# Selections, small S5 tables, splits on VectorE and a fourth PSUM bank for the a columns of a hybrid S5 and DeltaNet block

## The chip, the cores and the metric

The kernel runs on one core of a Trainium2 chip. The metric is the time on the device of one execution, in microseconds (us); lower is better.

## The reference

One block of a language model on 1024 tokens of width 1024, all in float32: an RMSNorm, one input projection, two branches side by side, an output projection, a gated addition and a last RMSNorm.

```python
a = rms_norm(h, norm_mix_g)
u_s, z_s, q, k, v, z_d, b_raw, a_raw = split(a @ w_in)      # 1024 x 3080
y_s = s5_branch(u_s, ...) * silu(z_s)                       # 32 groups of 16 channels, 64 states
y_d = gated_deltanet_branch(q, k, v, z_d, b_raw, a_raw, ...)  # 4 heads of 128
h = h + concat(y_s, y_d) @ w_out
h = h + sigmoid(h @ w_gate) * rms_norm(p @ w_ple, ple_norm_g)
return rms_norm(h, final_norm_g)
```

The decay of the DeltaNet branch is g = -exp(A_log) * softplus(a_raw + dt_bias), summed along the tokens and then exponentiated. So the four columns a_raw have to come out far more exactly than the rest. S5 is a diagonal state space with complex poles, which needs cosines and sines of multiples of an angle for each state.

## The kernel before

The engines are TensorE (PE in the profile), VectorE (DVE), ScalarE (ACT) and GpSimd (POOL); each works through its own queue in order. SyncE (SP) issues the transfers.

Float32 products are made of three matmuls in the rounded format fp32r: `mm3` multiplies high by high, high by low and low by high parts. `split(hi, lo, raw, e1, e2)` makes the parts: engine e1 copies raw into hi (rounding it), engine e2 subtracts, lo = raw - hi. The input projection goes in 24 weight tiles of 128 output columns (names u, q, k, v, d, z), each loaded by `wtile` into `wr` (one buffer) and split into `wh` and `wl` (two buffers each). The copy is on ACT; the subtraction is on POOL, but for the three tiles in EARLY, where DVE does it. A tile then takes 2 x 8 x 3 matmuls `pj` of 128x512.

The order on PE is written by the kernel itself. A planner keeps a clock of PE cost and a list of chains; each chain yields a number from the table LAT, the time that the other engines are expected to need until its next step, or the name of something that has to be done first. When no chain is due, the planner takes the next piece of filler, in the order of the string FILL: the projection tiles, then g (gram), l (the GLU of S5, matmuls `pg`), o (first half of the output projection, `po`), w, x (second half and the gate). The order on the other engines is made by the framework's scheduler, which lists instructions by a simulated timeline. Once made, all orders are fixed.

The stages, with the times of the profiled execution:

1. 0 to 67 us: the embedding product (`pe`, copied by ACT into e), the squares of x and their sums, `rms` (some fifty tiny DVE operations on the tile rsc), `scale_x` (8 DVE operations), then PE transposes x into `xtp`, and ACT and DVE split that into `ah` and `al`.
2. 67 to 515 us: the a columns (`a_chain`), with projection matmuls as filler and the four batches of S5 in between. The columns are cut into 64 units, 8 in each of 8 blocks b of 128 input channels. `a_prefix(n)`: 3 matmuls of the input by the tile `tg` (a column times a triangle) into a PSUM bank `pT`; ACT adds a large grid constant and writes `tb`, DVE subtracts neighbours back into the bank, ACT writes two more parts into a tile F. `a_sums(n - 2)`: 4 matmuls by `dg` (a column times the identity) onto the same bank, ACT evacuates it into F, four DVE scans (one for each head) add up, and the last sums go to `vst` (even b, an ACT copy) or `se` (odd b, a DVE subtraction). `diag(b)` makes dg and tg by four POOL products per block. The banks `pT` come from the pool MX (3 buffers); the pool MZ (2 buffers) serves S5, the transposes and others.
3. 515 to 660 us: `g_math` (g from the sums, DVE on 32 columns), its transpose `gtp` on PE, prefix sums in rows, `pe5` (PE brings gls and others back into columns, copied by DVE as `cols`), the decay matrices, the substitution that inverts the 32x32 blocks (`subst`, DVE), the doubling to 64 and 128 (`q32`, `d32`, `q64`).
4. 660 to about 780 us: eight chunks of the recurrence (banks `bk`, operands `ktp`, `kdec`, `rr`, `tq`, `v2`), with `pg` and `po` as filler.
5. To 956 us: the rest of `po`, transposes of h, the gate (`pq`), the output.

In an S5 batch (`s5_batch`), POOL builds the table s5tab of 128 cosines and sines for each state by doubling: seven steps of four dependent operations each.

Of the kernel before, what the change touches and what calls it, by code (L numbers as in the profile page):

```python
# [16 lines left out]
P = 128  # L17
# [8 lines left out]
def hymba_block_kernel(ctx: ExitStack, tc: tile.TileContext, A: dict, out: bass.AP, dbg=None):  # L26
# [10 lines left out]
    pm = ctx.enter_context(tc.tile_pool(name="pm", bufs=2, space=PSUM))  # L37
    ps = ctx.enter_context(tc.tile_pool(name="ps", bufs=1, space=PSUM))
    px = ctx.enter_context(tc.tile_pool(name="px", bufs=3, space=PSUM))
    pz = ctx.enter_context(tc.tile_pool(name="pz", bufs=2, space=PSUM))  # L40
    dr = ctx.enter_context(tc.tile_pool(name="dr", bufs=1, space=DRAM))

    def T(name, dt=F32, shape=None):
# [84 lines left out]
    def rsqrt(o, x, e=V):  # L128
        shp = list(x.shape)
        n = "rs" + "x".join(map(str, shp[1:]))  # L130
        hb = dp.tile(shp, I32, tag=n + "h", name="hb")
        t = dp.tile(shp, F32, tag=n + "t", name="rt")
        V.tensor_scalar(out=hb, in0=x.bitcast(I32), scalar1=1, scalar2=None, op0=ALU.logical_shift_right)
        ts(e, o.bitcast(I32), hb, -1.0, MUL, float(0x5F3759DF), ADD)
        for _ in range(3):
            stt(e, t, x, -0.5, o, MUL, MUL)
            tt(e, t, t, o, MUL)
            stt(e, o, t, 1.5, o, ADD, MUL)
# [176 lines left out]
    ud = dr.tile([4, 8, P, P], F32, name="ud")  # L315

    GRID = 24.0
    se = C("se", [P, 4, 8, 4])
    gridc = C("gridc", [P, 2])
    G.memset(gridc[:, 0:1], GRID)  # L320
    G.memset(gridc[:, 1:2], -GRID)
    FT = [fp.tile([P, FW], F32, tag="F", name=f"F{i}") for i in range(4)]
    wah, wal = C("wah", [P, 8, 4], F32R), C("wal", [P, 8, 4])
    V.tensor_copy(out=wah, in_=wba[:, :, 4:8])
    tt(V, wal, wba[:, :, 4:8], wah.bitcast(F32), SUB)

# [23 lines left out]
    rho8 = C("rho8", [P, 16])  # L350

    MAGIC = 12582912.0

    def s5_params():
        bc4 = TV("bc4", F32, [P, 4, 16, 16])
        SP.dma_start(out=bc4, in_=A["bc"])
        Br, Bi, Cr, Ci = (bc4[:, i] for i in range(4))
        pa = T("pa")
        pos = [0]

        def small(w=16):
# [29 lines left out]
        tt(V, k17, k17, k17, MUL)  # L391
        ts(V, pr, k17, -2.0, MUL, 1.0, ADD)
        en = [(small(), small())]
        V.tensor_copy(out=en[0][0], in_=pr[:, :, 8])
        V.tensor_copy(out=en[0][1], in_=pi[:, :, 8])
        tt(V, x17, lrdt.unsqueeze(2).to_broadcast([P, 16, 17]), lvb, MUL)
        act(k17, x17, AF.Exp)
        V.tensor_copy(out=rho8, in_=k17[:, :, 8])
        tt(V, pr, pr, k17, MUL)
        tt(V, pi, pi, k17, MUL)  # L400
        for i in range(1, 7):
            c0, s0 = en[-1]
# [58 lines left out]
    def s5_batch(b):  # L461
# [54 lines left out]
        V.memset(tab[:, 0, :, 0:1], 1.0)  # L516
        V.memset(tab[:, 1, :, 0:1], 0.0)
        for i in range(7):
            n = 1 << i
            cc = en[i][0][:, pp].unsqueeze(1).unsqueeze(3).to_broadcast([P, 2, 4, n])  # L520
            ss = en[i][1][:, pp].unsqueeze(1).unsqueeze(3).to_broadcast([P, 2, 4, n])
            tt(G, tab[:, :, :, n:2 * n], tab[:, :, :, 0:n], cc, MUL)
            tt(G, tb[:, :, :, 0:n], tab[:, :, :, 0:n], ss, MUL)
            tt(G, tab[:, 0, :, n:2 * n], tab[:, 0, :, n:2 * n], tb[:, 1, :, 0:n], SUB)
            tt(G, tab[:, 1, :, n:2 * n], tab[:, 1, :, n:2 * n], tb[:, 0, :, 0:n], ADD)
        yield f"u{b}"
        yield LAT["tab"]
        u = W("u", "p (g c) -> p g c", g=8)
# [59 lines left out]

    def half(w, hf, evac):
# [106 lines left out]
    def a_prefix(n):  # L696
# [20 lines left out]
    def a_sums(n):  # L717
# [7 lines left out]
            d0, d1 = (f[:, 384 * h + x:384 * h + 384:2] for x in range(2))  # L725
            V.tensor_tensor_scan(out=d0, data0=d0, data1=d1, initial=vst[:, i, h:h + 1] if hf else 0.0, op0=ADD, op1=ADD)  # L726
# [444 lines left out]
    def chunk(n):  # L1171
# [161 lines left out]
    def a_chain():  # L1333
        for n in range(66):
# [189 lines left out]
```

## Time and profile before

| | |
|---|---|
| median of 3 runs | 955.9 us (954.72 to 956.91) |
| the profiled execution | 957.75 us, span 956.0 us |
| mean granted clock of TensorE | 0.916 |
| busy: PE, DVE, ACT, POOL | 805.2, 709.2, 489.6, 343.4 us |

The profile gives start and duration of every instruction in one execution, and for an idle stretch of an engine what ended it ("<-"). A row of a group reads: line, engine, operation, written tile <- read tiles, shape, count | busy us, mean ns of one | idle before. A row of a stage gives its window, its length, the busy time of each engine with the number of instructions, the granted clock, and the load of the transfers. A row of the chain of work that ended last, or of the timeline, starts with the start and the duration in us.

### The profile page before, as it was taken

To read this page: it belongs to the slowest core of one execution; us is meant where nothing else is said; L and a number is where in the kernel's file an instruction comes from. 1 tells how busy PE (TensorE), PEld (TensorE's weight loads), DVE (VectorE), ACT (ScalarE), POOL (GpSimd) and SP (SyncE) were. 2 spreads that over 40 slices of the span, in tenths; PEclk is the share of its full clock that TensorE was granted. 3 is DMA by queue.
4 is the path that set the end of the run, shared out by engine and by line. 5 is a ranking of instruction groups with operands and counts; after the bars stand their busy time and mean duration, and the time that the engine had idled before them with its cause. 6 is when DMAs were issued, how large, how long until landed. Compare 5 with 4: busy or idle time off the path is not lost.

```text
span 956.0 us, 12315 instructions
## 1 busy us (share of the span) xinstructions
PE 805.2 (84%) x4338; PEld 649.1 (68%) x4338; DVE 709.2 (74%) x1478; ACT 489.6 (51%) x890; POOL 343.4 (36%) x326
## 2 busy tenths in 40 slices
PE   6479889877798976988998597599579999899996
PEld 3358468756686764876876376488467887778885
DVE  6946968988999878877548859953778754437886
ACT  7457667676696577766555244112355224113332
POOL 0120458676449348522102022101545219502222
PEclk9779989999899898998999798879789999999998
DMA  7430211403122031132102032104445534301211
GB/s 273 154 120 1 88 34 40 110 14 96 37 60 82 34 88 51 23 136 86 66 1 67 22 133 93 40 2 146 108 107 165 194 140 138 129 1 67 88 45 67
DMA packets 67581, 79.93 MB, mean 84 GB/s; under 512 B 23456, under 2 KB 49344, under 8 KB 67520
## 3 DMA queue, kind: packets, MB, share of 16 engines
q1 hardware_dynamic: 67376, 78.89, 25.9%
q8 instruction: 34, 0.56, 0.2%
q14 instruction: 27, 0.22, 0.1%
q10 hardware_dynamic: 144, 0.26, 0.1%
HBM read 57.39 MB, written 21.74 MB: 83 GB/s over the span
## 4 chain that ended last, share of the span: by engine, by line
PE 48%; DVE 27%; ACT 11%; issue 5%; DMA 5%; POOL 4%; SPq 1%; DVEq 0%; ACTq 0%; POOLq 0%
PE pj L111 16%; DVE F L726 9%; PE pq L111 9%; PE pT L111 6%; PE po L111 5%; ACT F L102 5%; DVE s5x L91 3%; PE bk L111 2%; DMA wr<-in_win 2%; DVE cv L99 2%; PE pg L111 2%; DVE pT L91 2%; ACT L102 1%; POOL wgl L91 1%; DVE s5x L554 1%
## 5 line engine op out<-in xcount | busy, mean ns | idle before, releaser
L111 PE MATMUL pj<-ah,wh 128*128 128x512 f32 x384 | 161.8, 421 | 12.3 <-ACT z L102 6.0
L111 PE MATMUL pj<-ah,wl 128*128 128x512 f32 x384 | 156.8, 408 | 0.7 <-POOL wl L91 0.7
L111 PE MATMUL pj<-al,wh 128*128 128x512 f32 x384 | 157.3, 410 | 0.0
L102 ACT ACTIVATE F<-F,gridc 128x512 f32<-128x512 f32 x128 | 115.2, 986 | 0.0
L91 POOL TENSOR_TENSOR wl<-wr,wh 128x1024 fp32r<-128x1024 f32 x21 | 52.2, 2485 | 137.6 <-ACT wh L102 137.6
L111 PEld LDWEIGHTS pj<-ah,wh 128*128 128x128 f32 x384 | 76.7, 200 | 31.9 <-ACT z L102 6.4
L111 PE MATMUL pT<-tg,ah 128*128 128x512 f32 x128 | 58.0, 453 | 47.0 <-ACT F L102 45.6
L726 DVE TENSOR_TENSOR_SCAN F<-F,vst 128x192 f32<-128x192 f32 x128 | 92.9, 784 | 3.2 <-ACT F L102 3.1
L726 DVE TENSOR_TENSOR_SCAN F<-F 128x192 f32<-128x192 f32 x128 | 85.7, 729 | 7.2 <-ACT F L102 7.1
L111 PEld LDWEIGHTS pj<-ah,wl 128*128 128x128 f32 x384 | 75.9, 198 | 19.5 <-POOL wl L91 1.2
L111 PEld LDWEIGHTS pj<-al,wh 128*128 128x128 f32 x384 | 76.4, 199 | 16.4
L91 DVE TENSOR_TENSOR pT<-F 128x512 f32<-128x512 f32 x64 | 51.0, 797 | 47.9 <-ACT F L102 46.4
L111 PEld LDWEIGHTS pT<-tg,ah 128*128 128x128 f32 x128 | 26.3, 205 | 60.7 <-ACT F L102 51.1
L111 PE MATMUL pq<-wgl,hth 128*128 128x512 f32 (+1 forms) x200 | 66.9, 386 | 0.0
L102 ACT ACTIVATE F<-pT 128x512 f32<-128x512 f32 x64 | 55.5, 867 | 2.1 <-PE pT L111 2.1
L99 DVE SCALAR_TENSOR_TENSOR cv<-raw,pk,cv 128x1023 f32<-128x1023 f32 (+2 forms) x36 | 52.9, 1470 | 3.9 <-ACT cv L102 3.8
L91 POOL TENSOR_TENSOR e<-e,pleg 128x1024 f32<-128x1024 f32 x8 | 19.3, 2412 | 97.7 <-ACT jq L102 88.3
L91 DVE TENSOR_TENSOR h<-h,po 128x512 f32<-128x512 f32 x32 | 21.9, 686 | 40.9 <-PE po L111 40.8
L102 ACT ACTIVATE F<-pT,tbl 128x128 f32<-128x128 f32 x128 | 36.5, 372 | 28.4 <-PE pT L111 28.3
L706 POOL COPY F<-tbl 128x4 f32<-128x4 f32 x32 | 16.5, 517 | 84.5 <-DVE pT L91 84.5
L102 ACT ACTIVATE wh<-wr 128x1024 fp32r<-128x1024 f32 x24 | 25.3, 1052 | 37.9 <-DMA wr<-in_win 14.9
L111 PE MATMUL pT<-dg,al 128*128 128x512 f32 x128 | 44.2, 429 | 0.0
(337 smaller groups left out, 2033.5 us busy)
## 6 DMA issues: line engine op xcount, KB each, us to landing
wr<-in_win SPq DMA_DIRECT2D x24, 512.0 KB, 3.7
x<-in_x SPq DMA_DIRECT2D x8, 512.0 KB, 8.1
wr<-in_wout SPq DMA_DIRECT2D x8, 512.0 KB, 4.0
h<-in_x SPq DMA_DIRECT2D x8, 512.0 KB, 4.6
wr<-in_wgate SPq DMA_DIRECT2D x8, 512.0 KB, 3.3
e<-ed SPq DMA_DIRECT2D x8, 512.0 KB, 3.2
out<-h SPq DMA_DIRECT2D x7, 512.0 KB, 2.6
ed<-e SPq DMA_DIRECT2D x6, 512.0 KB, 12.6
```

The lines of the kernel that those rows point to most:

```text
L91: return e.tensor_tensor(out=o, in0=a, in1=b, op=op)
L99: return e.scalar_tensor_tensor(out=o, in0=a, scalar=s, in1=b, op0=op0, op1=op1)
L102: return S.activation(out=o, in_=i, func=f, **k)
L111: return PE.matmul(o, lhsT=l, rhs=r, start=a, stop=z, **k)
L554: V.tensor_tensor_scan(out=flat(w[:, ri]), data0=flat(rh), data1=flat(v[:, ri]), initial=0.0, op0=MUL, op1=ADD)
L706: G.tensor_copy(out=tb[:, :, 0:1], in_=first)
L726: V.tensor_tensor_scan(out=d0, data0=d0, data1=d1, initial=vst[:, i, h:h + 1] if hf else 0.0, op0=ADD, op1=ADD)
```

## The change

Seven edits, in one diff:

1. Banks. The pool MZ becomes two tags, mz0 and mz1, with one buffer each. Units with n % 4 == 3 take mz1 (`own`), and from the first of them until the chain has ended all other users of MZ (S5's) get mz0. So the units rotate over four banks.
2. Selections. dg and tg of a block are made by one POOL `affine_select` each, from wap (high and low part of the columns in one tile), instead of two products each.
3. Tables. Two small tables of 16 and 8 entries for all 16 poles are built once in `s5_params` (28 small POOL operations); a batch makes its 128 entries from them by 8 POOL products and two sums.
4. All 24 subtractions of `wtile` are on DVE (21 were on POOL).
5. The sums of an odd block go to se2 by an ACT copy of the two last columns; one DVE subtraction in `g_math` replaces the 32 small ones.
6. rr, tq and v2 of a chunk lie in the tile of the small tables (rt4), and the scratch of the large `rsqrt` has one buffer.
7. Five numbers of LAT, which move filler on PE.

```diff
-    pz = ctx.enter_context(tc.tile_pool(name="pz", bufs=2, space=PSUM))
+    pz = ctx.enter_context(tc.tile_pool(name="pz", bufs=1, space=PSUM))
...
+    zi = [0, False]
+    def MZ(name, shape=None, own=False):
+        zi[0] = 1 if own else 0 if zi[1] else 1 - zi[0]
+        return pz.tile(shape or [P, 512], F32, tag=f"mz{zi[0]}", name=name)
...
     def diag(b):
-        sh = [P, 4, P]
         res = [T(f"{n}{b}", F32R, [P, 2, 4, P]) for n in ("dg", "tg")]
-        for x, w in enumerate((wah.bitcast(F32), wal)):
-            for o, m in zip(res, (ident, tri)):
-                tt(G, o[:, x], w[:, b, :].unsqueeze(2).to_broadcast(sh), m.unsqueeze(1).to_broadcast(sh), MUL)
+        w = wap[:, b].rearrange("p x h -> p (x h)").unsqueeze(2).to_broadcast([P, 8, P])
+        for o, c in zip(res, (ALU.is_equal, ALU.is_ge)):
+            G.affine_select(out=o.rearrange("p x h c -> p (x h) c"), in_=w, pattern=[[0, 8], [1, P]],
+                            compare_op=c, fill=0.0, base=0, channel_multiplier=-1)
...
+    def rotate(tb, x, i, c, s):
+        n = 1 << i
+        tt(G, tb[:, :, :, n:2 * n], tb[:, :, :, 0:n], c, MUL)
+        tt(G, x[:, :, :, 0:n], tb[:, :, :, 0:n], s, MUL)
+        tt(G, tb[:, 0, :, n:2 * n], tb[:, 0, :, n:2 * n], x[:, 1, :, 0:n], SUB)
+        tt(G, tb[:, 1, :, n:2 * n], tb[:, 1, :, n:2 * n], x[:, 0, :, 0:n], ADD)
...
-        prep=14.1, ev=3.3, scan=18.0, tab=8.7, g1=13.5, g2=10.6, dec=14.8, sub=14.7, blk=0.3,
-        q32=6.9, d32=6.5, q64=2.0, d64=0.8, kq=4.3, A=1.4, B=4.8, C=1.4, otp=10.3, vtp=23.2, ssq=30.3,
+        prep=14.1, ev=3.3, scan=18.0, tab=6.0, g1=23.0, g2=4.0, dec=14.8, sub=25.0, blk=0.3,
+        q32=6.9, d32=8.0, q64=2.0, d64=0.8, kq=4.3, A=1.4, B=4.8, C=1.4, otp=10.3, vtp=23.2, ssq=30.3,
...
-        for i in range(7):
-            n = 1 << i
-            cc = en[i][0][:, pp].unsqueeze(1).unsqueeze(3).to_broadcast([P, 2, 4, n])
...
+        for j in range(4):
+            lo = tbs[0][:, :, 4 * b + j].unsqueeze(2).to_broadcast([P, 2, 8, 16])
+            ch, sh_ = (tbs[1][:, r, 4 * b + j].unsqueeze(1).unsqueeze(3).to_broadcast([P, 2, 8, 16]) for r in range(2))
+            tt(G, t5[:, j:8:4], lo, ch, MUL)
+            tt(G, x5[:, j:8:4], lo, sh_, MUL)
+        tt(G, tab[:, 0], tab[:, 0], tb[:, 1], SUB)
+        tt(G, tab[:, 1], tab[:, 1], tb[:, 0], ADD)
...
-    EARLY = (12, 13, 16)
...
-        split(hi, lo, raw, S, V if mt in EARLY else G)
+        split(hi, lo, raw, S, V)
...
-        p = pxs[n] = MX("pT", [P, 4, P])
+        if n % 4 == 3:
+            zi[1] = True
+            p = pxs[n] = MZ("pT", [P, 4, P], True)
+        else:
+            p = pxs[n] = MX("pT", [P, 4, P])
...
-            tt(V, se[:, b // 2, i, :], f[:, 382:1536:384], f[:, 383:1536:384], SUB)
+            act(se2[:, b // 2, i], f[:, 0:1536].rearrange("p (h c) -> p h c", h=4)[:, :, 382:384], AF.Copy)
...
     def g_math():
+        se = FT[0][:, 0:128].rearrange("p (a b c) -> p a b c", a=4, b=8)
+        tt(V, se, se2[:, :, :, :, 0], se2[:, :, :, :, 1], SUB)
```

PE has 2728 instructions before and now, DVE 1152 and 1141, ACT 574 and 613, POOL 271 and 184; the transfers are 143 both times. ACT's two copies of the first weights stand where they stood: the first among the squares and the copies of e, the second behind the last copy of e. Three places where the order moves:

DVE, around the rms chain (tile rsc) and the scaling of x. Before, from the last sum of squares and, in the second piece, from the end of the chain:

```order
L188 SCALAR_TENSOR_TENSOR sq<-mask,sq 128x1024
L189 COPY rsc<-sq 128x16
L91 TENSOR_TENSOR rsc<-rsc 128x32 x3
L91 TENSOR_TENSOR rsc<-rsc 128x16
L91 TENSOR_TENSOR rsc<-rsc 128x8
```

```order
L91 TENSOR_TENSOR rsc<-rsc 128x8 x3
L99 SCALAR_TENSOR_TENSOR rsc<-rsc 128x8
L91 TENSOR_TENSOR rsc<-rsc 128x8
L99 SCALAR_TENSOR_TENSOR rsc<-rsc 128x8
L91 TENSOR_TENSOR rsc<-rsc 128x8
L95 TENSOR_SCALAR x_121<-x_121,rsc 128x1024 x2
```

Now, the same two places:

```order
L192 SCALAR_TENSOR_TENSOR sq<-mask,sq 128x1024
L193 COPY rsc<-sq 128x16
L95 TENSOR_TENSOR wl<-wr,wh 128x1024
L95 TENSOR_TENSOR rsc<-rsc 128x32 x3
L95 TENSOR_TENSOR rsc<-rsc 128x16
```

```order
L95 TENSOR_TENSOR rsc<-rsc 128x8
L103 SCALAR_TENSOR_TENSOR rsc<-rsc 128x8
L95 TENSOR_TENSOR rsc<-rsc 128x8
L95 TENSOR_TENSOR wl<-wr,wh 128x1024
L95 TENSOR_TENSOR rsc<-rsc 128x8 x2
L103 SCALAR_TENSOR_TENSOR rsc<-rsc 128x8
L95 TENSOR_TENSOR rsc<-rsc 128x8
L103 SCALAR_TENSOR_TENSOR rsc<-rsc 128x8
L95 TENSOR_TENSOR rsc<-rsc 128x8
L99 TENSOR_SCALAR x_121<-x_121,rsc 128x1024 x2
```

The first two subtractions of the weights (wl) stand in DVE's queue, the first ahead of the whole chain, the second ahead of its last six operations.

DVE, in the row form of g behind the transpose gtp: gls is the last row, F<-gls its spread, cols the copy of PE's pe5, vr the scaling of v. Before:

```order
L95 TENSOR_SCALAR F_407<-F_407 32x64
L96 TENSOR_SCALAR F_407<-F_407 32x64 x2
L91 TENSOR_TENSOR gls<-F_407 32x1
L849 COPY F_407<-gls 32x128
L91 TENSOR_TENSOR wl<-wr,wh 128x1024
L854 COPY cols<-pe_4266 128x64
L99 SCALAR_TENSOR_TENSOR cv<-raw,pk,cv 128x1023
L91 TENSOR_TENSOR em_4275<-em_4275,cols 128x8x64 x2
L91 TENSOR_TENSOR z_4276<-z_4276,cols 128x8x64 x2
```

Now:

```order
L100 TENSOR_SCALAR F_407<-F_407 32x64 x2
L95 TENSOR_TENSOR gls<-F_407 32x1
L95 TENSOR_TENSOR vr_3666<-vtp,sqk 128x2x128
L95 TENSOR_TENSOR vr_3667<-vtp,sqk 128x2x128
L872 COPY F_407<-gls 32x128
L877 COPY cols<-pe_4255 128x64
L95 TENSOR_TENSOR vr_3668<-vtp,sqk 128x2x128
L95 TENSOR_TENSOR vr_3669<-vtp,sqk 128x2x128
L95 TENSOR_TENSOR wl<-wr,wh 128x1024
```

The subtraction between gls and cols is gone from there. On PE, 48 projection matmuls stood between gtp and pe5, and now 18; between the last sums of the a columns and gtp there were 54, and now 126.

PE, from the transposes of k for the first chunk (ktp) to the chunk's first matmuls (bk); pj is the input projection, pg the GLU. Before:

```order
L115 MATMUL ktp<-cm,k_3638 128x128 x4
L111 MATMUL pj<-ah_140,wh 128x512
L111 MATMUL pj<-al_148,wh 128x512
L111 MATMUL pj<-ah_140,wl 128x512
L111 MATMUL pj<-ah_141,wh 128x512
L111 MATMUL pj<-al_149,wh 128x512
L111 MATMUL pj<-ah_141,wl 128x512
L111 MATMUL pj<-ah_142,wh 128x512
L111 MATMUL pj<-al_150,wh 128x512
L111 MATMUL pj<-ah_142,wl 128x512
L111 MATMUL bk<-vr_3752,zt_3646 128x128 x4
L111 MATMUL pj<-ah_135,wh 128x512
```

Now:

```order
L119 MATMUL ktp<-cm,k_3552 128x128 x4
L115 MATMUL pg<-gh_4910,wgh 128x512
L115 MATMUL pg<-gl_4909,wgh 128x512
L115 MATMUL pg<-gh_4910,wgl 128x512
L115 MATMUL pg<-gh_4910,wgh 128x512
L115 MATMUL pg<-gl_4909,wgh 128x512
L115 MATMUL pg<-gh_4910,wgl 128x512
L115 MATMUL pg<-gh_4917,wgh 128x512
L115 MATMUL pg<-gl_4916,wgh 128x512
L115 MATMUL pg<-gh_4917,wgl 128x512
L115 MATMUL bk<-vr_3666,zt_3560 128x128 x4
L115 MATMUL pg<-gh_4917,wgh 128x512
```

The projection has ended before this place, and the GLU stands there. In all, 303 projection matmuls stood between the last sums of the a columns and the first bk; now 336 do, and 45 of the GLU besides, so 78 fewer of these big matmuls come behind it. Chunk 6 is left with 15 matmuls of filler, and behind the last chunk's output 102 matmuls po remain, where there were 198.

More of the change, by code (lines that the diff above doesn't have):

```diff
@@ L82, in MX @@
         return px.tile(shape or [P, 512], F32, tag="mx", name=name)
-    def MZ(name, shape=None):
-        return pz.tile(shape or [P, 512], F32, tag="mz", name=name)
+    zi = [0, False]
+    def MZ(name, shape=None, own=False):
+        zi[0] = 1 if own else 0 if zi[1] else 1 - zi[0]
+        return pz.tile(shape or [P, 512], F32, tag=f"mz{zi[0]}", name=name)
     def MS(name, shape=None):
@@ L130, in rsqrt @@
         n = "rs" + "x".join(map(str, shp[1:]))
-        hb = dp.tile(shp, I32, tag=n + "h", name="hb")
-        t = dp.tile(shp, F32, tag=n + "t", name="rt")
+        hb = dp.tile(shp, I32, tag=n + "h", name="hb", bufs=3 if shp[1] < 32 else 1)
+        t = dp.tile(shp, F32, tag=n + "t", name="rt", bufs=3 if shp[1] < 32 else 1)
         V.tensor_scalar(out=hb, in0=x.bitcast(I32), scalar1=1, scalar2=None, op0=ALU.logical_shift_right)
@@ L317, in hymba_block_kernel @@
     GRID = 24.0
-    se = C("se", [P, 4, 8, 4])
+    se2 = C("se2", [P, 4, 8, 4, 2])
     gridc = C("gridc", [P, 2])
@@ L322, in hymba_block_kernel @@
     FT = [fp.tile([P, FW], F32, tag="F", name=f"F{i}") for i in range(4)]
-    wah, wal = C("wah", [P, 8, 4], F32R), C("wal", [P, 8, 4])
-    V.tensor_copy(out=wah, in_=wba[:, :, 4:8])
-    tt(V, wal, wba[:, :, 4:8], wah.bitcast(F32), SUB)
+    wap = C("wap", [P, 8, 2, 4], F32R)
+    V.tensor_copy(out=wap[:, :, 0], in_=wba[:, :, 4:8])
+    tt(V, wap[:, :, 1], wba[:, :, 4:8], wap[:, :, 0].bitcast(F32), SUB)
     def diag(b):
-        sh = [P, 4, P]
         res = [T(f"{n}{b}", F32R, [P, 2, 4, P]) for n in ("dg", "tg")]
-        for x, w in enumerate((wah.bitcast(F32), wal)):
-            for o, m in zip(res, (ident, tri)):
-                tt(G, o[:, x], w[:, b, :].unsqueeze(2).to_broadcast(sh), m.unsqueeze(1).to_broadcast(sh), MUL)
+        w = wap[:, b].rearrange("p x h -> p (x h)").unsqueeze(2).to_broadcast([P, 8, P])
+        for o, c in zip(res, (ALU.is_equal, ALU.is_ge)):
+            G.affine_select(out=o.rearrange("p x h c -> p (x h) c"), in_=w, pattern=[[0, 8], [1, P]],
+                            compare_op=c, fill=0.0, base=0, channel_multiplier=-1)
         return res
@@ L352, in hymba_block_kernel @@
     MAGIC = 12582912.0
+    rt4 = C("rt4", [P, 8, P])
+    rtf = rt4.rearrange("p a b -> p (a b)")
+    tbs = [rtf[:, a:z].rearrange("p (r j n) -> p r j n", r=2, j=16) for a, z in ((0, 512), (512, 768))]
+    tbx = rtf[:, 768:1024].rearrange("p (r j n) -> p r j n", r=2, j=16)
+    def rotate(tb, x, i, c, s):
[4 more added lines that the diff above has]
+        tt(G, tb[:, 1, :, n:2 * n], tb[:, 1, :, n:2 * n], x[:, 0, :, 0:n], ADD)
     def s5_params():
@@ L408, in s5_params @@
             en.append((c1, s1))
+        for tb, e0, n in ((tbs[0], 0, 4), (tbs[1], 4, 3)):
+            V.memset(tb[:, 0, :, 0:1], 1.0)
+            V.memset(tb[:, 1, :, 0:1], 0.0)
+            for i in range(n):
+                c0, s0 = (e.unsqueeze(1).unsqueeze(3).to_broadcast([P, 2, 16, 1 << i]) for e in en[e0 + i])
+                rotate(tb, tbx, i, c0, s0)
         nr, den, cr, ci, t16 = (small() for _ in range(5))
@@ L515, in s5_batch @@
         tb = W("x2", "p (r j c) -> p r j c", r=2, j=4)
-        V.memset(tab[:, 0, :, 0:1], 1.0)
-        V.memset(tab[:, 1, :, 0:1], 0.0)
-        for i in range(7):
-            n = 1 << i
-            cc = en[i][0][:, pp].unsqueeze(1).unsqueeze(3).to_broadcast([P, 2, 4, n])
[L521 to L525, printed above, removed]
+        t5, x5 = (t.rearrange("p r j (m n) -> p (r j) m n", n=16) for t in (tab, tb))
+        for j in range(4):
[5 more added lines that the diff above has]
+        tt(G, tab[:, 1], tab[:, 1], tb[:, 0], ADD)
         yield f"u{b}"
@@ L1191, in chunk @@
                 mm(bk[:, 2, :], ksl(qq, n, h), Sst[h])
-                rr = dp.tile([P, P], F32, tag="rr", name="rr", bufs=4)
+                rr = rt4[:, h]
                 stt(V, rr, bk[:, 0, :], neg[:, ucs[h]], vr[c][:, i, h, :], MUL, ADD)
-                tq = dp.tile([P, P], F32, tag="tq", name="tq", bufs=4)
+                tq = rt4[:, 4 + h]
                 act(tq, bk[:, 2, :], AF.Copy, scale=eg[:, ucs[h]])
@@ L1202, in chunk @@
             mm(bks[h][:, 1, :], zu(4 * n + h), rrs[h])
-            v2 = rrs[h] if n else dp.tile([P, P], F32, tag="rr", name="v2", bufs=4)
+            v2 = rrs[h] if n else rt4[:, h]
             ts(V, v2, bks[h][:, 1, :], dd[:, ucs[h]], MUL)
@@ L1343, in a_chain @@
         yield 8.0
+        zi[1] = False
         done.add("a")
```

## The prediction

> **What bounds the kernel now.** I read the page's first part, then the table by stage, the waits of PE and of ScalarE (ACT), the groups by form, the chain that ended last, and the timeline where the change moves something. All sums start from the profiled execution, 957.75 us around a span of 956.0 us; it is 1.85 us above the median of the three runs, 955.9 us, and I take that off at the end. About 0.2% (1.9 us) is what a measurement here can tell from no change.
>
> ```profile
> PE 805.2 (84%) x4338; PEld 649.1 (68%) x4338; DVE 709.2 (74%) x1478; ACT 489.6 (51%) x890; POOL 343.4 (36%) x326
> 90.00:520.00 430.00, 369.94 (x1923) 294.58 (x1921) 352.92 (x555) 295.18 (x520) 211.33 (x240) 0.93 0.21 61
> 520.00:660.00 140.00, 108.66 (x847) 88.69 (x848) 100.92 (x244) 36.19 (x54) 17.06 (x10) 0.84 0.20 67
> 660.00:780.00 120.00, 101.46 (x580) 86.13 (x579) 88.30 (x247) 50.03 (x127) 48.91 (x29) 0.91 0.47 140
> 780.00:956.00 176.00, 163.06 (x763) 134.02 (x761) 108.69 (x311) 54.83 (x122) 54.24 (x27) 0.97 0.24 83
> ```
>
> The columns of a stage are its length and the busy time of PE, its weight loads, DVE, ACT and POOL. The 64 units of the a columns fill 90 to 520 us: PE idles 60 of 430 us there, DVE 77. From 520 to 660 (g, decay, substitution, doubling) PE idles 31 us of 140, and only 13 of 176 us at the end.
>
> ```profile
> 127.00:180.00 53.00, 48.18 (x282) 38.52 (x283) 43.35 (x65) 36.36 (x71) 33.76 (x49) 0.94 0.20 53
> 180.00:233.00 53.00, 41.87 (x234) 32.60 (x233) 47.31 (x64) 38.17 (x63) 38.28 (x48) 0.96 0.30 73
> 233.00:287.00 54.00, 47.76 (x239) 38.97 (x238) 50.24 (x72) 42.20 (x79) 23.66 (x26) 0.94 0.17 50
> 287.00:341.00 54.00, 47.75 (x293) 38.46 (x292) 48.40 (x62) 33.84 (x56) 37.92 (x41) 0.94 0.22 66
> 341.00:397.00 56.00, 42.60 (x237) 34.02 (x238) 46.54 (x70) 41.17 (x76) 33.59 (x44) 0.91 0.21 55
> 397.00:457.00 60.00, 53.44 (x249) 43.38 (x248) 44.46 (x74) 41.45 (x65) 16.75 (x14) 0.91 0.28 97
> 457.00:511.00 54.00, 50.26 (x243) 42.34 (x242) 30.65 (x55) 34.29 (x69) 6.78 (x6) 0.94 0.12 40
> ```
>
> Each row is a block of eight units, b = 1 to 7. The busier of PE and DVE adds up to 48.18 + 47.31 + 50.24 + 48.40 + 46.54 + 53.44 + 50.26 = 344.4 us of 384. So 39.6 us are lost because PE, ACT and DVE wait for one another, and DVE is the busier one in four blocks. Where PE loses it:
>
> ```profile
> PE pT L111 <- ACT F L102: 45.6, 17, 6.9
> ACT vst L102 <- DVE F L726: 55.7, 21, 5.3
> L111 PE MATMUL pT<-tg,ah 128*128 128x512 f32 x128 | 58.0, 453 | 47.0 <-ACT F L102 45.6
> ```
>
> Nearly all of it stands before the tg matmul, a unit's first, which needs a free PSUM bank; ACT's evacuation of three units ago releases it. ACT, in its turn, waits for DVE's scans.
>
> **The a stage: banks, splits, selections, tables.** The fourth bank lets that matmul wait for the evacuation of four units ago, one unit (about 53/8 = 6.6 us) more slack, against waits of at most 6.9 us. What remains is what DVE and ACT themselves can do.
>
> ```profile
> L91 POOL TENSOR_TENSOR wl<-wr,wh 128x1024 fp32r<-128x1024 f32 x21 | 52.2, 2485 | 137.6 <-ACT wh L102 137.6
> L91 DVE TENSOR_TENSOR wl<-wr,wh 128x1024 fp32r<-128x1024 f32 x3 | 3.6, 1216 | 10.1 <-ACT wh L102 10.1
> L91 DVE TENSOR_TENSOR se<-F 128x4 f32<-128x4 f32 x32 | 10.5, 328 | 0.5
> L726 DVE TENSOR_TENSOR_SCAN F<-F,vst 128x192 f32<-128x192 f32 x128 | 92.9, 784 | 3.2 <-ACT F L102 3.1
> L726 DVE TENSOR_TENSOR_SCAN F<-F 128x192 f32<-128x192 f32 x128 | 85.7, 729 | 7.2 <-ACT F L102 7.1
> 110.99 4.87 DVE L726 TENSOR_TENSOR_SCAN F<-F 128x192 f32<-128x192 f32 x4
> 112.35 2.65 POOL L91 TENSOR_TENSOR wl<-wr,wh 128x1024 fp32r<-128x1024 f32 x1
> 131.33 1.91 DVE L726 TENSOR_TENSOR_SCAN F<-F 128x192 f32<-128x192 f32 x4
> 90.00:520.00 430.00, 37.56 (x15) 0.93 0.21 61
> ```
>
> (The last row is POOL's wl alone.) Four scans take 1.91 us, but 4.87 us when POOL works on two SBUF operands at the same time. 64 groups at 1.91 us would be 122 us; they took 92.9 + 85.7 = 178.6, so about 57 us of DVE's time is collision with POOL's 211 us, 0.27 us for each.
>
> - Splits: 15 leave POOL in this stage, -37.56 us there, and cost DVE 15 x 1.216 = +18.2.
> - Diagonals: four products of 1.19 to 1.38 us each (5.12 us together; two of the four groups are shown), per b, become two selections. The nearest row is a selection of the same 128x1024, 1.68 us: 8 x (5.12 - 3.36) = -14 us of POOL.
>
> ```profile
> L91 POOL TENSOR_TENSOR tg<-wal,cm 128x512 fp32r<-128x512 f32 x8 | 11.1, 1383 | 0.0
> L91 POOL TENSOR_TENSOR tg<-wah,cm 128x512 fp32r<-128x512 f32 x8 | 9.6, 1194 | 2.0 <-PE pT L111 2.0
> L970 POOL TENSOR_SCALAR_AFFINE_SELECT em<-em 128x1024 f32<-128x1024 f32 x3 | 5.0, 1678 | 28.8 <-DVE em L91 28.8
> ```
>
> - Tables: 28 dependent products and sums per batch become 10, plus 28 small ones once. I call it -14 us of POOL (an estimate; bounds 0 and -40); nothing waits for them.
> - So POOL falls by about 66 us and DVE's collisions by 66 x 0.27 = -18. Dropping se gives -10.5. With the splits DVE ends about 10 us lower; a split on POOL was the longest collider and cost more than the mean, so I take -15, bounds 0 and -25. The one subtraction 128x128 in g_math and the new memsets are under 1 us.
> - se2 on ACT: 32 copies, which now wait for the scans in odd b too, as vst does in even b. The blocks tell the price: odd b lasted 53, 54, 56, 54 us, even b 53, 54, 60. So 0 to 6 us; I take 1 inside the figure below.
> - S5's second tile on one bank: its partner (MS) has one bank already, and every S5 step already waits for that: 0.
>
> With DVE 4.3% lower the busier engine sums to about 338 us. I let the fourth bank recover half of the 39.6 us, since it removes PE's wait but not ACT's for DVE: 338 + 20 = 358, a gain of 384 - 358 = **27**. Bounds: overhead unchanged, 7; overhead gone, 46.
>
> **The head: two splits ahead of the rms chain.** On DVE the first split now stands ahead of the rms chain, and the second ahead of its last six operations.
>
> ```profile
> 41.32 1.06 ACT L102 ACTIVATE wh<-wr 128x1024 fp32r<-128x1024 f32 x1 [10.45 <-DMA wr<-in_win]
> 52.78 1.05 ACT L102 ACTIVATE wh<-wr 128x1024 fp32r<-128x1024 f32 x1
> 33.48 0.93 DVE L91 TENSOR_TENSOR rsc<-rsc 128x32 f32<-128x32 f32 x5
> 41.52 7.51 DVE L95 TENSOR_SCALAR x<-x,rsc 128x1024 f32<-128x1024 f32 x8
> 52.09 1.12 PE L115 MATMUL xtp<-cm,x 128*128 128x128 f32 x8
> ```
>
> The weights release ACT's first copy, which ends at 42.4, so the first split ends at 43.6 and the chain (33.48 to 41.52, 8.0 us) moves behind it, to 51.6. ACT's second copy stands behind all copies of e and ends at 53.8; the second split ends at 55.05, the last six operations at about 56.3, the four scalings that the first transposes need (4 x 0.94) at 60.0. PE's transposes began at 52.09: **+8**. Bounds: +3.3 if only the first split decides (51.6 + 3.75 - 52.09), +9.
>
> **The middle: g to the first chunk.**
>
> ```profile
> PE gtp L115 <- DVE gg L91: 10.8, 1, 10.8
> PE q L111 <- DVE q L1048: 10.7, 1, 10.7
> 515.38 4.20 DVE F L726 x4
> 271.05 4.18 PE pj L111 x18
> 550.94 0.21 DVE L849 COPY F<-gls 32x128 f32<-32x128 f32 x1
> 561.11 1.23 DVE L91 TENSOR_TENSOR wl<-wr,wh 128x1024 fp32r<-128x1024 f32 x1 [9.96 <-ACT wh L102]
> ```
>
> PE waited 10.8 us for gg. Now 126 in-projection matmuls stand between the last sums and gtp, instead of 54; at 4.18/18 = 0.232 us the 72 more take 16.7 us, so the hole closes and gtp comes some 3 us later (+3; DVE, with a split of 1.2 us among g's operations, arrives about then). Behind it, DVE idled 9.96 us because a split stood between gls and the copy of cols, waiting for ACT. That split is gone from there, and pe5 stands behind 18 projection matmuls, not 48: 30 x 0.232 = 7 us earlier (-7). Two splits on POOL that stretched DVE operations in the decay and the substitution are gone: -4, bounds 0 and -6. Together **-8**, bounds 0 and -14.
>
> **Behind the first chunk.** 33 more projection matmuls and 45 of the GLU now stand ahead of the first bk, so 78 x 0.232 = 18.1 us of PE work leave the part that comes after it. Ahead of it they fit: PE was busy 109 of 140 us there, 109 + 18 = 127 within 140 - 8 = 132. From 18 I take 4, for one chunk (n = 6) that is left with hardly any filler: **-14**, bounds 0 and -22.
>
> **A rule weighed.** A split that starts on DVE while POOL reads is itself late: a DVE operation on 231 columns lasted 2.46 us beside POOL's 2.43.
>
> ```profile
> 607.48 2.43 POOL L91 TENSOR_TENSOR wl<-wr,wh 128x1024 fp32r<-128x1024 f32 x1 [10.26 <-ACT wh L102]
> 607.70 2.46 DVE L91 TENSOR_TENSOR xt<-q,q 128x231 f32<-128x231 f32 x1
> ```
>
> POOL keeps some 145 of 430 us, 34%, in pieces as long as the selection's 1.68 us, half of which is left on average: 15 x 0.34 x 0.8 = +4, against nothing in my sum, as the three splits on DVE took 1.2 us each. The Trainium skill, "SBUF — State Buffer", section "Who interferes with whom", says that a DVE instruction with two SBUF inputs contends with a GpSimd instruction that reads SBUF, and that the later one is fully blocked; by it the sum would be 4 us higher, and the selections, which read SBUF too, would not be free of collisions.
>
> **Sum.** +8 - 27 - 8 - 14 = -41: 957.75 - 41 = 916.75, less 1.85: **915 us**.
>
> **Rivals.**
> - DVE and ACT hold the a stage (0.14): overhead unchanged, gain 7: 935. For it: ACT waited 55.7 us for scans, and now has twice as many copies behind scans. Against: odd and even blocks were alike.
> - The overhead goes (0.15): the stage follows the busier engine, gain 46: 896. For it: PE's wait stands at one place, the bank.
> - Slower (0.15, of it 0.03 within 0.2%): a split on DVE waits for ACT's copy, which waits for its weights or for PE to free a buffer, and every scan stands behind it. The three of before idled 10.1 us, 3.4 each; 19 new ones behind the head, all felt, are 19 x 3.4 = 64: 979. It decides from 41/19 = 2.2 us each. Against it: two of the three waited 0.1 us together.
> - Splits blocked by POOL, as weighed (0.07): 919.
> - The matmuls that were pulled ahead only lengthen the middle, and the change doesn't do there what its new figures say (0.07): 915 + 14 = 929.
>
> My forecast (903 to 927) has 0.42. Faster: 0.42 + 0.14 + 0.15 + 0.07 + 0.07 = 0.85; same 0.03; slower 0.12. Eight in ten lie between the second rival's 896 with its own few us and the first one's 935 with some waits of the third: 890 to 945.
>
> **What would show it.** Right: xtp begins near 60; PE's wait pT for ACT F falls below 20 us; the last sums of the stage near 515 + 8 - 27 = 496; no DVE idle of 10 us ahead of cols; PE idle of 520 to 660 shrinks to some 10 us. Wrong: DVE idle ahead of wl of more than 2 us each (third rival), ACT's wait for scans near 100 us (first), or PE waiting for gh or gl ahead of the first bk (last).

## The result, and the profile after

The median of four runs is 925.1 us (923.4 to 927.9), against 955.7 us (954.7 to 956.9) before: a ratio of 0.968, 95% interval 0.966 to 0.971. The time lies in the range of the prediction (890 to 945), and the gain is 31 us where 41 were forecast. The profiled execution has a span of 922.9 us, 33 less than before's 956.0. The busy times, from the page of the changed kernel:

```profile
PE 794.8 (86%) x4338; PEld 641.1 (69%) x4338; DVE 701.2 (76%) x1464; ACT 491.8 (53%) x922; POOL 255.6 (28%) x245
```

I cut both spans at the same events: the first tg matmul of the a columns, the last dg matmul, the first bk, the last transpose of a chunk's output (otp), the end. The table by stage, first of the changed kernel, then of before:

```profile
75.20:515.60 440.40, 385.79 (x2004) 310.03 (x2005) 345.18 (x556) 307.55 (x566) 140.33 (x172) 0.92 0.20 58
515.60:652.10 136.50, 121.83 (x938) 99.23 (x937) 112.03 (x266) 55.69 (x79) 26.33 (x15) 0.94 0.37 112
652.10:789.90 137.80, 124.45 (x687) 103.94 (x685) 104.99 (x273) 50.01 (x135) 58.68 (x34) 0.96 0.40 132
789.90:922.90 133.00, 120.07 (x577) 99.07 (x575) 92.33 (x277) 38.95 (x97) 26.33 (x14) 0.98 0.16 59
```

```profile
67.10:516.20 449.10, 390.53 (x2003) 311.38 (x2004) 361.08 (x580) 307.22 (x539) 211.93 (x246) 0.93 0.20 58
516.20:659.50 143.30, 109.66 (x853) 89.11 (x852) 104.61 (x249) 38.15 (x57) 19.53 (x11) 0.85 0.19 65
659.50:799.70 140.20, 121.42 (x676) 102.37 (x674) 99.36 (x272) 57.03 (x141) 58.03 (x34) 0.93 0.45 138
799.70:956.00 156.30, 143.59 (x673) 118.28 (x670) 97.75 (x285) 48.12 (x109) 45.12 (x22) 0.97 0.22 77
```

The head is 8.1 us longer (67.1 to 75.2). The a stage is 8.7 us shorter, the middle 6.8, the chunks 2.4, and the end behind them 23.3. Two thirds of the gain is one number: 96 matmuls po fewer behind the last chunk (x673 to x577), 96 x 0.232 = 22.3 us.

**The head**, from the timeline of DVE and of PE:

```profile
42.68 1.23 DVE L95 TENSOR_TENSOR wl<-wr,wh 128x1024 fp32r<-128x1024 f32 x1 [8.36 <-ACT wh L106]
54.16 1.23 DVE L95 TENSOR_TENSOR wl<-wr,wh 128x1024 fp32r<-128x1024 f32 x1 [3.41 <-ACT wh L106]
56.37 5.39 DVE L99 TENSOR_SCALAR x<-x,rsc 128x1024 f32<-128x1024 f32 x8
61.68 1.40 DVE L103 SCALAR_TENSOR_TENSOR al<-xtp,pk,ah 128x512 fp32r<-128x512 f32 x2
57.18 0.49 PE L119 MATMUL xtp<-cm,x 128*128 128x128 f32 x1 [4.63 <-DVE x L99]
62.48 1.98 PE L119 MATMUL xtp<-cm,x 128*128 128x128 f32 x8 [1.97 <-DVE al L103]
```

The same second group of transposes before:

```profile
55.24 1.41 PE L115 MATMUL xtp<-cm,x 128*128 128x128 f32 x8 [2.04 <-DVE al L99]
```

DVE stands 8.36 us for ACT's first copy with the rms chain behind it, and 3.41 us for the second with six operations left. The scaling is quicker than in the sum (5.39 us against 7.51, since no POOL subtraction runs beside it), so PE starts on x at 57.2, not 60: 5.1 us later than before (52.09). The rest of the delay comes behind that. PE's second group of transposes waits for DVE's first al, and al stands in DVE's queue behind all eight scalings; that group is 7.2 us late (55.24 to 62.48), and the first tg matmul 8.1 us.

**The a stage.** The wait that the fourth bank was to remove is gone, 45.6 us down to 1.9. Other waits stand in its place. The waits of PE, then those of ACT, from 75 to 515 us:

```profile
PE kps L115 <- ACT s5h L106: 10.4, 4, 5.3
PE kps L115 <- POOL F L727: 7.6, 1, 7.6
PE yps L115 <- POOL s5x L95: 7.2, 3, 5.7
...
PE hp L119 <- DVE s5x L95: 4.8, 2, 3.3
PE pj L115 <- DVE ssq L905: 4.8, 2, 3.0
PE pj L115 <- ACT se L106: 3.9, 1, 3.9
...
PE pT L115 <- ACT F L106: 1.9, 1, 1.9
```

```profile
ACT vst L106 <- DVE F L747: 49.1, 24, 6.0
ACT se L106 <- DVE F L747: 43.7, 19, 6.5
ACT F L106 <- PE pT L115: 28.3, 13, 4.3
```

PE now waits at S5's steps (hp, kps, yps) and for evacuations of its other banks. The 7.6 us that the view puts down to POOL also end behind ACT: its copies of hp begin at 371.18 us, and PE goes on at 371.94. ACT waits 93 us for scans, where it was 56. One place shows the link; ACT, DVE and PE at 278 to 291 us:

```profile
278.62 0.21 ACT L106 ACTIVATE se<-F 128x8 f32<-128x8 f32 x1 [2.45 <-DVE F L747]
284.69 0.21 ACT L106 ACTIVATE se<-F 128x8 f32<-128x8 f32 x1 [5.86 <-DVE F L747]
...
289.95 0.58 ACT L106 ACTIVATE s5h<-hp 128x512 f32<-128x512 f32 x1
```

```profile
278.51 2.38 DVE L103 SCALAR_TENSOR_TENSOR cv<-raw,pk,cv 128x1022 f32<-128x1022 f32 x1
280.82 1.79 DVE L95 TENSOR_TENSOR pT<-F 128x512 f32<-128x512 f32 x1
282.52 2.14 DVE L747 TENSOR_TENSOR_SCAN F<-F,vst 128x192 f32<-128x192 f32 x4
...
290.14 2.14 DVE L747 TENSOR_TENSOR_SCAN F<-F,vst 128x192 f32<-128x192 f32 x4 [2.35 <-ACT F L106]
```

```profile
290.67 0.60 PE L115 MATMUL kps<-s5ca,bb 64*32 64x128 f32 x2 [5.29 <-ACT s5h L106]
```

ACT stands 5.86 us at a copy of last sums, because DVE does a convolution step and a subtraction before the scans. Behind that copy on ACT are the two copies out of a projection bank, a table load of 1.28 us, an operation of 1.06 us on cv, and the evacuations of the next unit and of S5's hp. PE waits 5.29 us for the last, and DVE itself 2.35 us for the next unit's F.

**The middle and the end.** PE no longer waits 10.8 us at gtp and 10.7 us at q32. Behind 515 us its longest waits are these:

```profile
PE bk L115 <- ACT rt L106: 7.2, 7, 2.0
PE vtp L119 <- ACT z L106: 6.4, 1, 6.4
PE po L115 <- DVE h L95: 4.3, 3, 3.1
```

### The profile page after: what moved, and what is told of

Its sections match the earlier page's. It is cut to its first block, busy times and chain, and to the rows that moved or that the text cites. A ratio compares the mean times of both kernels' runs of the same rounds, so it can differ in the third digit from the quotient of the medians.

```text
span 922.9 us, 12230 instructions
## 1 busy us (share of the span) xinstructions
PE 794.8 (86%) x4338; PEld 641.1 (69%) x4338; DVE 701.2 (76%) x1464; ACT 491.8 (53%) x922; POOL 255.6 (28%) x245
## 5 line engine op out<-in xcount | busy, mean ns | idle before, releaser
L115 PE MATMUL pj<-ah,wh 128*128 128x512 f32 x384 | 159.6, 416 | 18.0 <-ACT z L106 5.3
L747 DVE TENSOR_TENSOR_SCAN F<-F,vst 128x192 f32<-128x192 f32 x128 | 85.9, 731 | 11.7 <-ACT F L106 11.6
L747 DVE TENSOR_TENSOR_SCAN F<-F 128x192 f32<-128x192 f32 x128 | 74.1, 639 | 17.5 <-ACT F L106 17.4
L115 PEld LDWEIGHTS pj<-al,wh 128*128 128x128 f32 x384 | 75.2, 196 | 16.2
L115 PE MATMUL pT<-tg,ah 128*128 128x512 f32 x128 | 55.6, 435 | 4.0 <-POOL tg L335 2.1
L727 POOL COPY F<-gridc 128x4 f32<-128x4 f32 x32 | 12.3, 385 | 159.2 <-DVE pT L95 87.4
L103 DVE SCALAR_TENSOR_TENSOR cv<-raw,pk,cv 128x1023 f32<-128x1023 f32 (+2 forms) x36 | 49.9, 1386 | 0.1
L95 DVE TENSOR_TENSOR wl<-wr,wh 128x1024 fp32r<-128x1024 f32 x24 | 30.9, 1286 | 20.5 <-ACT wh L106 20.5
L115 PE MATMUL pT<-dg,ah 128*128 128x512 f32 x128 | 42.6, 416 | 0.5 <-DVE pT L95 0.5
L115 PEld LDWEIGHTS pq<-wgl,hth 128*128 128x128 f32 x200 | 37.0, 188 | 7.4
L727 POOL COPY F<-tbl 128x4 f32<-128x4 f32 x32 | 13.2, 411 | 102.9 <-DVE pT L95 97.0
```

The lines of the kernel that those rows point to most:

```text
L95: return e.tensor_tensor(out=o, in0=a, in1=b, op=op)
L103: return e.scalar_tensor_tensor(out=o, in0=a, scalar=s, in1=b, op0=op0, op1=op1)
L115: return PE.matmul(o, lhsT=l, rhs=r, start=a, stop=z, **k)
L727: G.tensor_copy(out=tb[:, :, 0:1], in_=first)
```

## The experiments

Twelve kernels ran, all timed against the kernel before, which had medians of 955.7 to 956.2 us beside them. "The changed kernel" is 925.1 us. The intervals of the ratios reach 0.2 to 0.4% to each side, 2 to 4 us, so a difference of some 4 us between two kernels is at the edge of what these runs can tell. Each edit was undone or done by itself, but for the sixth (the tiles of a chunk), which was not tried alone.

### The copies of the last sums

```diff
-            act(se2[:, b // 2, i], ..., AF.Copy)
+            tt(V, se[:, b // 2, i, :], f[:, 382:1536:384], f[:, 383:1536:384], SUB)
```

> The changed kernel, but the last sums of odd blocks go to se by a DVE subtraction again (32 of about 0.2 to 0.33 us), not by an ACT copy. Theory A, ACT's queue: the copies make ACT stand in its own order for the scans (43.7 us of waits in the a stage), S5's evacuations s5h<-hp stand behind them, and PE waits for those at kps. Then the waits of PE at kps fall from 18 us to under 8, the last sums come at 500 to 508 instead of 514.9, and the time is 910 to 918 against 925. Theory B, DVE holds the stage: 7 to 10 us more work on DVE make the stage longer, 930 to 935.

It took 914.4 us (909.2 to 917.9; ratio 0.956, 0.952 to 0.959): 10.7 us less. The last sums came at 501.9 us, in a profiled execution of 909.2 us. ACT's waits in the a stage:

```profile
ACT vst L106 <- DVE F L747: 59.0, 25, 6.4
ACT F L106 <- PE pT L115: 34.6, 20, 4.6
ACT cv L106 <- DVE cv L103: 14.9, 5, 7.7
```

Theory A holds, with more work on DVE in the a stage (351.0 us against 345.2) and less time. But PE's wait at kps fell from 18.0 to 13.4 us only, not below 8, so that one step carries part of it. Others fell too (yps from 7.2 to 4.1, the projection's wait behind the copies se from 3.9 to none), and the wait at pT for ACT rose from 1.9 to 5.3.

The same for the other half of the units, on top of it:

```diff
-            act(vst[:, i, :], f[:, 382:1536:384], AF.Copy)
+            V.tensor_copy(out=vst[:, i, :], in_=f[:, 382:1536:384])
```

> Both copies of the last sums on DVE: se by a subtraction, vst by a copy of four columns, right behind the scans on their own engine. ACT then waits for no scan (59 us of waits in the kernel with se alone on DVE), and DVE gets 32 operations of 0.2 to 0.33 us more. Theory A, the two queues waiting for each other: last sums by 495, time 902 to 910. Theory B, by now DVE holds the stage: 914 to 920.

908.1 us (905.2 to 910.0; ratio 0.950, 0.947 to 0.954), 6.3 us less again, last sums at 494.3. ACT's waits for scans are gone:

```profile
ACT F L106 <- PE pT L115: 55.6, 27, 8.2
ACT cv L106 <- DVE cv L103: 29.0, 7, 8.6
```

Now ACT waits mostly for PE, which is the busiest engine; 29 us for DVE's convolutions remain.

### The fourth bank

```diff
-        if n % 4 == 3:
-            zi[1] = True
-            p = pxs[n] = MZ("pT", [P, 4, P], True)
-        else:
-            p = pxs[n] = MX("pT", [P, 4, P])
+        p = pxs[n] = MX("pT", [P, 4, P])
```

(and MZ with two rotating buffers, as before.)

> The changed kernel with the pools of before: the a units over three banks, S5's second tile over the two MZ banks again. If the fourth bank is worth what the vanished wait says, part of 45.6 us, the wait pT for ACT F comes back with 30 to 45 us and the time is 935 to 950. If the wait has only moved to S5's steps (kps, yps, hp, together 30 us) and to evacuations, then pT's wait comes back, theirs go, and the time is 921 to 930. If S5's single bank costs more than the fourth bank brings, it is below 921.

928.6 us (923.3 to 930.3; ratio 0.970, 0.967 to 0.974): the bank is worth 3.5 us here, within what these runs can tell from nothing. PE's waits in the a stage:

```profile
PE pT L111 <- ACT F L102: 37.1, 17, 4.9
PE pT L111 <- POOL tg L331: 5.6, 2, 4.9
PE gps L111 <- DVE zt L91: 3.1, 2, 1.8
```

The wait at pT is back with 37.1 us, and those at kps and yps are gone from the list: the second theory, the waits had only moved. The edit does two things, though: it takes the fourth bank from the units and gives S5 its second bank back. No run separates them, but the traces bound the second. In the changed kernel, 1.73 and 1.39 us of the waits at kps stand between ACT's first and second copy of hp, at the one MZ bank that is left to S5; with three banks for the units, the kps matmuls of the third batch began at 291.21 us, before that second copy (291.31 us), and ran through without a wait. Most of the 18.0 us stands at the first copy, whose bank was single before too. Whether ACT's copies hid the bank's worth was asked without them:

> Sums of odd blocks on DVE and only three banks for the a units, S5 on two MZ banks. The fourth bank brought 3.5 us beside the ACT copies. If those copies were what hid its worth, it is worth 10 to 20 us here: 924 to 934 against 914.4 with four banks. If the bank only moves PE's waits to S5's steps in any case: 912 to 919.

918.5 us (914.7 to 924.7; ratio 0.962, 0.958 to 0.966) against 914.4 with four banks: 4.1 us. So it is small in both cases. PE waited 38.9 us at pT there, and 5.3 us with the fourth bank (e1's trace), for 4 us of time.

### The subtractions of the weights

```diff
+    EARLY = (12, 13, 16)
...
-        split(hi, lo, raw, S, V)
+        split(hi, lo, raw, S, V if mt in EARLY else G)
```

> The changed kernel, but 21 of the 24 weight subtractions are on POOL again. The head: xtp begins at 52 instead of 57 to 60, 8 us less in every theory. In the a stage DVE loses 15 x 1.29 = 19 us of subtractions and gets about 20 us of collisions back. Theory A (the waits between ACT and DVE hold the stage): no net effect there, and the hole ahead of cols may come back, so 917 to 926. Rival: the subtractions on DVE, which wait for ACT's copies, were what ate the gain of the fourth bank; then the stage is 10 to 20 us shorter and the time 898 to 908.

934.4 us (931.9 to 939.5; ratio 0.978, 0.975 to 0.981), 9.4 us more, though the first tg matmul came at 66.4 instead of 75.2. The a stage took 447.9 us instead of 440.4, and from the last sums to the first bk it was 144.0 instead of 136.5. The rival is out, and the first theory's 917 to 926 was missed as well. DVE's own time doesn't explain it: it was busy for 345.1 us of the a stage, against 345.2, so the collisions with POOL (scans 165.3 us against 160.0, convolution steps and others longer) cost DVE what the subtractions would. What grew are waits of PE in the a stage, for POOL's tg from 2.1 to 8.7 us and for the projection's evacuations into z from 4.9 to 10.7. Why they grew was not separated. The first two subtractions cost something on DVE:

```diff
-        split(hi, lo, raw, S, V)
+        split(hi, lo, raw, S, G if mt in (20, 21) else V)
```

> The changed kernel, but the first two weight subtractions, those ahead of and inside the rms chain, are on POOL. By the head's reckoning xtp begins at 52 instead of 57 and the first pT at 67 instead of 75.2, and all later stages follow 8 us earlier: 916 to 919. Rival: a later stage waits for something that does not move with the head (S5's chain, loads), and takes part of it back: 921 to 925.

921.7 us (913.3 to 923.7; ratio 0.962, 0.958 to 0.966): 3.4 us less, while the first tg matmul came 8.1 us earlier (67.1) and the last sums 5.5 (510.1). So the a stage took 2.6 us back. With the sums of odd blocks on DVE:

> Sums of odd blocks on DVE (914.4 alone) and the first two subtractions on POOL (921.7 alone, 3.4 under the changed kernel). If the 8 us of the head are taken back by S5's steps while ACT stands for the scans, they are felt more fully once it does not: 905 to 908. If something else takes them back (DVE's load, loads of weights), the two only add: 910 to 913.

907.5 us (906.1 to 907.9; ratio 0.950, 0.946 to 0.953), 6.9 us under the 914.4 of that kernel. The first theory is the nearer one, but 3.4 and 6.9 differ by little more than the runs can tell.

### Selections and tables

The next kernel has the four POOL products per block again (edit 2 undone).

> The changed kernel with dg and tg made by four POOL products per block again, 14 us more work on POOL in all. By the prediction's collisions (0.27 us of DVE for each us of POOL) DVE gets 4 us more, of which the end sees a part: 925 to 930. Rival: the products come later than the selections, and PE, which waited 2.1 us for tg, waits more: 930 to 938.

930.4 us (926.4 to 933.2; ratio 0.972, 0.970 to 0.975), 5.4 us more, at the border of the two theories; PE waited 5.6 us for tg instead of 2.1. The scans took 170.6 us, 10.6 more than the changed kernel's 160.0:

```profile
L747 DVE TENSOR_TENSOR_SCAN F<-F,vst 128x192 f32<-128x192 f32 x128 | 92.9, 785 | 7.2 <-ACT F L106 6.8
L747 DVE TENSOR_TENSOR_SCAN F<-F 128x192 f32<-128x192 f32 x128 | 77.7, 667 | 18.9 <-ACT F L106 18.8
```

So of the three edits to POOL's work this one did most for the scans; the end saw half of it.

In the next one POOL doubles S5's tables in every batch again (edit 3 undone).

> The changed kernel with S5's tables made by doubling in each batch again, some 14 us more work on POOL in 28 dependent steps. Collisions alone: 4 us of DVE, 925 to 930. Rival: with the planner's shorter figure for the table (6.0 against 8.7) S5's steps come before their tables and PE waits for them: 930 to 940.

917.7 us (915.8 to 920.9; ratio 0.960, 0.958 to 0.963): 7.4 us *less*. Neither theory said so. POOL was busy for 153.9 us between 75.2 and 514.9, against 140.3 in the changed kernel, yet the scans were not slower. The scans by form, of the changed kernel and then of this one:

```profile
L747 DVE TENSOR_TENSOR_SCAN F<-F,vst 128x192 f32<-128x192 f32 x128 | 85.9, 731 | 11.7 <-ACT F L106 11.6
L747 DVE TENSOR_TENSOR_SCAN F<-F 128x192 f32<-128x192 f32 x128 | 74.1, 639 | 17.5 <-ACT F L106 17.4
```

```profile
L743 DVE TENSOR_TENSOR_SCAN F<-F,vst 128x192 f32<-128x192 f32 x128 | 83.3, 710 | 11.4 <-ACT F L106 11.3
L743 DVE TENSOR_TENSOR_SCAN F<-F 128x192 f32<-128x192 f32 x128 | 73.4, 633 | 16.9 <-ACT F L106 16.9
```

The new tables are products of 0.8 us and sums of 1.66 us; these are the sums:

```profile
L95 POOL TENSOR_TENSOR s5tab<-s5tab,s5x 128x512 f32<-128x512 f32 x8 | 13.1, 1660 | 0.1
```

The doubling's steps are mostly of 8 to 128 columns and 0.5 us. PE's wait at kps also fell, from 18.0 us to 6.7. Whether the collisions or the order of the queues made the 7.4 us was not separated. In the scans the difference is only (85.9 + 74.1) - (83.3 + 73.4) = 3.3 us, no more than between kernels with the same work on POOL (157.4 us with three banks, 161.5 with the first two subtractions on POOL). In all, DVE was busy for 335.6 us of the a stage, 9.6 less than the changed kernel's 345.2; those with three banks, with the first two subtractions on POOL and with the old figures had 342.9, 345.1 and 348.3.

### The planner's figures

```diff
-        tab=6.0, g1=23.0, g2=4.0, dec=14.8, sub=25.0, ... d32=8.0
+        tab=8.7, g1=13.5, g2=10.6, dec=14.8, sub=14.7, ... d32=6.5
```

> The changed kernel with the five figures of the planner as before, so PE's order is that of before. If the gain behind the first chunk (25 us) is filler that the new figures pulled ahead, the first two chunks stand without filler again, 198 matmuls po come behind the last chunk, and the time is 945 to 953. If it came from the freed DVE and POOL instead, 925 to 935.

949.4 us (946.2 to 950.5; ratio 0.993, 0.991 to 0.996): the five figures are worth 24.4 us of the 30.7. From the first bk to the end it took 295.2 us, before 296.5, the changed kernel 270.8. The two holes are back in PE's waits, and 673 matmuls stand behind the last chunk again, as before the change:

```profile
PE q L115 <- DVE q L1071: 12.1, 1, 12.1
PE gtp L119 <- DVE gg L95: 10.0, 1, 10.0
792.80:948.80 156.00, 143.70 (x673) 118.22 (x671) 97.67 (x285) 48.16 (x109) 45.24 (x22) 0.98 0.22 77
```

The other way round, the kernel before with the five figures alone:

> The kernel before with only the five figures of the planner changed. If the 24 us that the figures are worth in the changed kernel depend on nothing else: 928 to 935. If they need what the other edits freed (no subtraction between gls and cols, fewer collisions in the decay), the filler that is pulled ahead makes the middle longer, and 940 to 955 remain.

937.4 us (936.3 to 940.8; ratio 0.981, 0.979 to 0.983), a gain of 18.8, between the two expectations. Its last stage:

```profile
800.00:934.50 134.50, 121.46 (x577) 100.35 (x575) 92.37 (x277) 38.95 (x97) 26.34 (x14) 0.96 0.16 59
```

Behind the first bk it took 271.5 us, as in the changed kernel; the middle took 142.7 us, where the changed kernel needs 136.5 and before 143.3. So the gain behind the first chunk needs nothing else, and the 7 us of the middle need both. The figures alone shorten the way from gtp to the first bk to 104.5 us, but gtp comes 38.2 us behind the last sums (34.4 in the changed kernel, 31.6 before), and PE waits 3.9 us there for DVE.

### The version that beats both

Both copies of the last sums on DVE and the first two subtractions on POOL.

> Both copies of the last sums on DVE (908.1 alone) and the first two subtractions on POOL (6.9 us beside se on DVE). If they add, as queue waits at different places should: 900 to 903. If DVE, which by now has the work of both, holds the stage, less than half of it comes: 905 to 908.

901.1 us (900.1 to 902.2; ratio 0.942, 0.940 to 0.944), 7.0 us under the kernel without the second edit: they add. It is 24 us faster than the changed kernel. With the old tables it was not run.

## Why the prediction was right, and where it was not

- **The head, +8: right in size, in part by another path.** +8.1 us at the first tg matmul. The two waits are those that were named, but they delayed the start of the transposes by 5.1 us, not 8; the rest came because al stands behind all eight scalings, where the sum counted four. Undoing it gave 3.4 us, or 6.9 without the ACT copies; the stages behind take part of it back.
- **The a stage, -27: the term that was mis-sized; -8.7 measured.** DVE's part came out as summed: 361.1 to 345.2 us, -15.9 (I took -15), and the scans lost 178.6 - 160.0 = 18.6 us of collision (-18). The parts of that total were not as summed. Undone one at a time, the splits changed DVE's busy time in the stage by nothing, the selections by 8.8 us (354.0), se2 by 5.8 (351.0), and the tables by 9.6 the other way (335.6); these don't add up to 15.9, so it is partly luck that the total agrees. The last line of the sum, 384 - 358, is 26; unrounded, 337.5 + 19.8 leaves a gain of 26.7. The step that failed is "the fourth bank recovers half of the 39.6 us". It removed nearly all of PE's wait at the bank and was worth 3.5 to 4.1 us. The wait had a cause behind it, ACT's late evacuations, and PE met the same lateness at the next bank it needed. "S5's second tile on one bank: 0" failed too, on a small scale: 3.1 us of PE's waits at kps stand at that bank. The second large step is "se2 on ACT: 0 to 6 us; I take 1": 10.7 us. I bounded it by the lengths of odd and even blocks, but a block's length also holds its splits, convolutions and S5 steps, and these can hide the difference. My first rival (gain 7, for "ACT has twice as many copies behind scans") describes this stage, and its sign came, ACT's wait for scans near 100 us (93); the last sums came at 515.6 us, not near 496.
- **The middle, -8: right** (-6.8). gtp came 34.4 us behind the last sums instead of 31.6 (+2.8, +3 forecast), and from gtp to the first bk it took 102.1 us instead of 111.7 (-9.6; -11 forecast). DVE copied cols 5.4 us behind gtp instead of 14.4, so the split that is gone from there and the shorter way to pe5 brought 9.0 us, not 7. The 4 us for splits on POOL in the decay came to some 2.5: the kernels that have them on POOL with the new figures took 104.8 and 104.5 us from gtp to the first bk. The filler that was pulled ahead took some 2 us back (from the copy of cols on, 99.2 us with the figures alone, 97.2 before).
- **Behind the first chunk, -14: mis-sized, -25.7 measured** (2.4 + 23.3). I counted 78 matmuls fewer there and took 4 off for a chunk without filler. But the chunks kept as many matmuls as before (x676 and x687) and took about as long (140.2 and 137.8 us): filler from behind them moved up into their gaps. So what counts is what is left behind the last one, 96 matmuls fewer. The count stood in the order, and I used the wrong one.
- **The rule weighed, +4: too large.** The 24 subtractions on DVE took 1.286 us on average, against 1.216. Only three of them started while POOL was at work, and took 2.09, 1.57 and 1.57 us; the others took 1.20 to 1.23. That is 1.6 us in all. The Trainium skill, "SBUF — State Buffer", section "Who interferes with whom", has the later instruction wait for the whole of the earlier; the three agree with it, each lasting longer by about what POOL's operation had left.
- **The slower rival: out.** In the a stage, DVE waited 5.9 us in 7 places for ACT's copies of weights, 0.8 each; it would have taken 2.2 each of 19.

With the four stages as measured, the sum reads +8 - 9 - 7 - 26 = -34, and the profiled execution came out 33.1 us shorter (924.7 against 957.75). That the forecast of -41 lies so near is in part luck: the a stage brought 18 us less than forecast, and the part behind the first chunk 12 us more.

## What to carry to other kernels

A wait at a buffer is worth what its releaser can deliver: before adding a buffer, ask why the release is late, since the producer meets the same late engine at its next buffer, and from whom the buffer is taken. An instruction that has to wait for another engine costs its own queue all that stands behind it: 32 copies of 0.2 us on ACT cost 10.7 us in all, and the same work right behind its source on DVE was cheaper although DVE was the busier of the two. Where a chain has filler in its gaps, work that is pulled ahead of the chain comes off its end, as later filler moves up: count the filler that is left when the chain has ended.

## What the hardware showed that I had not expected

POOL's total busy time does not set DVE's loss. The tables by doubling kept POOL busy 13.6 us longer between 75.2 and 514.9 us, and DVE's busy time in the a stage was 9.6 us shorter; the four products per block kept POOL busy 19.0 us longer, and DVE's was 8.8 us longer. The doubling is made mostly of steps of about 0.5 us, the products take 1.2 to 1.3 us; whether their length is the reason was not tested. And the scaling of x, a tile times one number for each partition, was slowed by POOL's subtraction too: eight of them took 5.39 us alone and 7.51 us beside it.
